# A two-layer hybrid backbone with experts: rooms of 32 rows for the two lightest experts of the second layer

## The chip, the cores and the metric

One core of one Trainium2 chip. The metric is the device time in us of one execution; a lower one is better. The profiled execution is one such execution, seen by the hardware profiler: its span runs from the first to the last of the program's instructions. TensorE is called PE in the rows, its weight loads PEld, VectorE DVE, ScalarE ACT, GpSimd POOL and SyncE SP.

## What is computed

Two layers over 512 latent tokens and, in the first layer, 256 context tokens, 1024 channels each, all in float32. A layer is a mixer (a bidirectional RWKV branch and a Hyena branch) and then a mixture of experts. The change is in the experts of the second layer, on 512 tokens. Cut to that:

```python
scores = softmax(h @ w_router); sel = scores + router_bias
best_group = argmax over 4 groups of (sum of the group's two best sel)
idx = top 2 of sel inside the best group;  wts = scores[idx] / their sum
y[t] = sum over i in 0, 1 of wts[t, i] * ((silu(h[t] @ w_gate[e]) * (h[t] @ w_up[e])) @ w_down[e])   # e = idx[t, i]
x = layer_norm(ALPHA * x + gate * y)
```

There are 16 experts, each with three matrices of 1024 x 1024, 12.6 MB in float32. All of them are read from HBM, 201 MB in the second layer. Which tokens go to which expert is known only at run time. On these inputs the reference's routing of the second layer gives expert 0 62 tokens and the others, from the heaviest, 170, 114, 90, 75, 75, 74, 60, 55, 47, 44, 39, 33, 29, 29 and 28.

## The kernel before

*Ranks and rooms.* Expert 0 is rank 0 and is computed first. The other 15 are sorted at run time by their number of tokens: rank 1 is the heaviest, rank 15 the lightest. CAPS (L25) gives each rank a room, a fixed number of rows; in the second layer 64 for rank 0, 192, 128, five times 96 (ranks 3 to 7) and eight times 64 (ranks 8 to 15). Tokens that find no place in their expert's room go to blocks of 128 rows, each computed by a loop at the end (`overflow`), which runs as often as there are such blocks: here not at all. NOVF (L68) is the most of such blocks that any routing can need.

*Turns.* TURN (L26) says which ranks are computed together. The second layer has seven turns: rank 0 alone (T0), then rank 1 with the pair (15, 14) (T1), 2 with (13, 12) (T2), 3 with (11, 10) (T3), 4 with 5 (T4), 6 with 7 (T5), and the pair (9, 8) (T6). The two experts of a pair share one unit of rows: one gather, one tile of operands, one write of results. A unit has at most 128 rows, so rank 1 with 192 rows is two units. In a turn the experts go forward in six steps: gate, up, gate, up (each for one half of the hidden channels), then two down steps (each for one half of the output channels). Each expert of the turn does one chunk of the step after the other; a chunk reads one block of weights of 1024 x 512.

*Weights.* A chunk's block comes as two halves of 1 MB (`weights`, L2145, tile `raw`), one DMA each from SyncE's queue, into ten buffers in turn (RAW, L23). SyncE's queue is in order: a half is asked for when its buffer is free and when the semaphore that will tell of its landing is free again; every half is read once. So the weights are a stream of 192 halves in the order of the turns.

*Matmuls.* The stationary operand is 128 channels x w rows of tokens, the moving one the weights, in float32. Pieces of 128 rows use the whole array. A piece of 64 rows puts the two halves of the moving columns into two column groups of the array, and one of 32 rows four quarters into four (L1997); in a down chunk the column groups take turns over the contraction instead (L2000). A 96-row expert is a piece of 64 and one of 32. The trace shows two matmul records for each call, as float32 takes. The results of gate and up are multiplied and transposed back (`turned`, L2043). After a down chunk the column groups have to be added up: `total` copies one half of the partitions (ScalarE, L2053) and adds it to the other (VectorE, L2054); for 32 rows it does so a second time (L2058, L2059). Then the rows are scaled (L2119).

*Results.* In all turns but the last the rows are written to a buffer in DRAM by ScalarE's queue (yd<-y, L2126), in rooms of 128 rows a unit. The last turn's are added through a matmul with a selection matrix (L2094, L2095), and while it runs GpSimd gathers each token's rows from the DRAM buffer (`early`, L1821). The rooms' unused rows in that buffer are set to zero at the start (`zero_unused`, L684). Operands of a turn are gathered by GpSimd (xg<-hd,idx, L1921) and transposed by TensorE (L1939) in the turn before.

*What sets the order.* Every engine runs its own list of instructions in order; the list is fixed when the program is built, and the build may move an instruction past others that do not depend on it. The two pieces of a 96-row expert, one after the other in the code, alternate by half chunks in the trace.

Of the kernel before, what the change touches and what calls it, by code (L numbers as in the profile page):

```python
# [8 lines left out]
F32 = mybir.dt.float32  # L9
# [3 lines left out]
ALU = mybir.AluOpType  # L13
# [8 lines left out]
NTOK, NCTX, NLAT = 768, 256, 512  # L22
RAW = 6, 10  # L23
AHEAD = 2, 2
CAPS = ([96] + [256] + [192] + [160] * 3 + [96] * 3 + [64] * 7, [64] + [192] + [128] + [96] * 5 + [64] * 8)  # L25
TURN = ([((0,),), ((1,), (15, 14)), ((2,), (13, 12)), ((3,), (11, 10)), ((4,), (6,)), ((5,), (7,)), ((8,), (9,))],  # L26
        [((0,),), ((1,), (15, 14)), ((2,), (13, 12)), ((3,), (11, 10)), ((4,), (5,)), ((6,), (7,)), ((9, 8),)])
LATE = 1, 1
XLO = (1, 3), ()
EARLY_V = ()  # L30
# [11 lines left out]
def most_overflow(caps, slots, most):  # L42


    seen = {}

    def go(r, n, left):
        if r < 1:
            return 0
        key = (r, n, left)  # L50
        if key not in seen:
            best = 0
            for b in range(0, (most - caps[r] + 127) // 128 + 1):
                m = max(n, caps[r] + 128 * (b - 1) + 1 if b else 0)
                if m > min(most, left):
                    break
                best = max(best, -(-max(0, m - caps[r]) // 128) + go(r - 1, m, left - m))
            seen[key] = best
        return seen[key]

    best = 0
    for b in range((most - caps[0] + 127) // 128 + 1):
        m = caps[0] + 128 * (b - 1) + 1 if b else 0
        best = max(best, b + go(len(caps) - 1, 0, slots - m))
    return best


NOVF = (most_overflow(CAPS[0], 2 * NTOK, NTOK), most_overflow(CAPS[1], 2 * NLAT, NLAT))  # L68


def rows_of(l):


    base, q, first = {}, 0, 0
    cut = max(0, len(TURN[l]) - LATE[l])
    for i, group in enumerate(TURN[l]):
        first = q if i == cut else first
        for ranks in group:
            for j, r in enumerate(ranks):
                base[r] = 128 * q + 64 * j  # L80
            q += -(-CAPS[l][ranks[0]] // 128)
    return [base[r] for r in range(16)], q, first


NSB = tuple(rows_of(l)[1] for l in range(2))
P_BMOD, P_MU, P_W0, P_A0, P_KK, P_KA, P_RK, P_CW, P_CB, P_HB, P_LG, P_LB, P_NG, P_NB = 0, 48, 63, 71, 79, 83, 87, 91, 127, 139, 143, 147, 151, 159
NPAR = 167
# [36 lines left out]
def shape_constants():  # L124
# [47 lines left out]
    for l in range(2):  # L172
        caps[:, l, 0] = CAPS[l]
        caps[:, l, 1] = rows_of(l)[0]
# [404 lines left out]
class Kern:  # L579
# [37 lines left out]
    def setup(self):  # L617
# [40 lines left out]
        self.hd = self.dt_([NTOK, 1024], "hd")  # L658
        self.xd = self.dt_([6, 128, 1024], "xd")
        self.yd = [self.dt_([128 * rows_of(l)[2] + 1, 1024], f"yd{l}") for l in range(2)]  # L660

    def layer(self, l):
# [21 lines left out]
    def zero_unused(self, pool):  # L684
# [4 lines left out]
        for l in range(2):  # L689
            base, nsb, first = rows_of(l)  # L690
            used = {(b + 32 * i) // 32 for b, c in zip(base, CAPS[l]) for i in range(c // 32)}
            for q in range(4 * first):
# [908 lines left out]
    def moe(self, l, st):  # L1601
# [5 lines left out]
        nb = 6 - b0  # L1607
        caps = CAPS[l]
        nblk = [-(-c // 128) for c in caps]
# [344 lines left out]
    def expert(self, l, P, evs, units, xs):  # L1954
# [4 lines left out]
        nc, A = self.nc, self.A  # L1959
        tt, stt = nc.vector.tensor_tensor, nc.vector.scalar_tensor_tensor  # L1960
        n = len(evs)
        pieces = []
        for u, (rows, *_) in enumerate(units):
            split = self.splits(l, rows, n)
            if n == 2:
                pieces += [(u, 64, 64 * j, j, False) for j in range(2)]
            elif rows == 128:
                pieces.append((u, 128, 0, 0, split))
            else:
                pieces += [(u, 64, 0, 0, False)] * (rows >= 64) + [(u, 32, rows // 64 * 64, 0, False)] * (rows % 64 > 0)  # L1970
# [78 lines left out]

        def total(a, w, o):  # L2050

            t = P["a"].tile([128, 512], F32, name="sum", tag="y", bufs=3)[o:o + 64]
            nc.scalar.copy(t, a[64 - o:128 - o])  # L2053
            tt(t, a[o:o + 64], t, ALU.add)  # L2054
            if w == 64:
                return t
            v = P["a"].tile([128, 512], F32, name="sum", tag="y", bufs=3)[o:o + 32]
            nc.scalar.copy(v, t[32:64])  # L2058
            tt(v, t[0:32], v, ALU.add)  # L2059
            return v  # L2060

        def select(u):
# [38 lines left out]
        def down(h, j):  # L2101
            H = slice(512 * h, 512 * h + 512)

            def done(acc):
                for u, (rows, _, own, dst, _) in enumerate(units):
                    if j == 0:
                        out[u] = P["a"].tile([128, 512], F32, name="y", tag="yw", bufs=YW[l])
                        if l == 0:
                            g[u] = P["a"].tile([128, 512], F32, name="g", tag="act", bufs=ACT_BUFS[l])
                            stt(g[u][0:rows], self.grow[1][0:rows, H], own[:, 2:3], self.grow[0][0:rows, H], ALU.mult, ALU.add)  # L2110
                        else:
                            g[u] = self.grow[0][:, H]
                for (u, w, o, *_), a in zip(mine[j], acc):
                    rows, _, own, dst, _ = units[u]
                    R = slice(o, o + w)
                    y, by = out[u][R], own[R, 1:2]
                    if w < 128:
                        a = total(a, w, o)
                    stt(y, a, by, g[u][R], ALU.mult, ALU.mult)  # L2119
                if j < n - 1:  # L2120
                    return
                for u, (rows, _, own, dst, _) in enumerate(units):
                    if dst is None:
                        add(u, h)
                    else:
                        nc.scalar.dma_start(dst[:, H], out[u][0:rows])  # L2126
            return done
# [94 lines left out]
```

## Time and profile before

| | us |
|---|---|
| three runs, median (lowest, highest) | 3251.6 (3239.0, 3257.0) |
| profiled execution | 3243.5 |
| its span | 3241.7 |
| TensorE busy | 2926.6, 90% |
| VectorE, ScalarE, GpSimd busy | 1661.5, 1119.7, 569.0 |
| T1 to T6 and close of the second layer's experts | 538 |

A busy TensorE is not one at its peak: matmuls are pipelined, and the records of the four column groups lie over each other. A group of rows by form gives busy time as the union of its records, so busy time by count is what one record adds. A wait for several semaphores is put down to the one that came last.

### The profile page before, as it was taken

The numbers are of one execution on the slowest core, as the hardware profiler recorded it, in microseconds if no ns is written. First come the engines' busy times: TensorE is split into PE (matmuls) and PEld (weight loads), VectorE is DVE, ScalarE is ACT, GpSimd is POOL, SyncE is SP. The second block draws the span as 40 slices with busy tenths as digits, with TensorE's granted clock in tenths as the row PEclk, the third lists the DMA queues.
The fourth block names the chain that finished last, engine by engine and source line by source line (L and its number), as shares of the span: only waits on it lengthen the run. The fifth ranks groups of instructions, "written<-read, shape, count | busy, mean of one in ns | idle before, by whom it ended". The sixth has DMA issues, their size and how long they took to land. (4 is left out here: it accounts for less than half of the span.)

```text
span 3241.7 us, 60246 instructions
## 1 busy us (share of the span) xinstructions
PE 2926.6 (90%) x24658; PEld 2002.0 (62%) x24658; DVE 1661.5 (51%) x2971; ACT 1119.7 (35%) x2275; POOL 569.0 (18%) x456
## 2 busy tenths in 40 slices
PE   7999999888988799999997999989989879999994
PEld 5877866676777566555652867646666665444551
DVE  4466534887766544435645347446886570111223
ACT  3454225656421133333422444254564221111110
POOL 1001222444004200000022001254440030000002
PEclk8999999899999799999997899987999979999998
DMA  5453274111244689998895464451112549999996
GB/s 223 126 155 103 80 257 143 45 54 49 100 136 169 244 341 367 361 361 320 320 359 213 150 200 120 158 173 57 42 59 75 188 189 377 362 410 421 379 374 248
DMA packets 221345, 689.49 MB, mean 213 GB/s; under 512 B 71877, under 2 KB 99814, under 8 KB 169608
## 3 DMA queue, kind: packets, MB, share of 16 engines
q1 hardware_dynamic: 186280, 587.57, 49.2%
q10 hardware_dynamic: 26960, 71.65, 6.3%
q0 software_dynamic: 7824, 26.36, 2.2%
q8 instruction: 197, 3.23, 0.4%
q14 instruction: 84, 0.69, 0.1%
HBM read 621.20 MB, written 64.30 MB: 211 GB/s over the span
## 5 line engine op out<-in xcount | busy, mean ns | idle before, releaser
L1997 PE MATMUL acc<-raw,x 128*64 128x256 f32 (+2 forms) x6656 | 556.4, 339 | 19.9 <-DMA raw<-in_w_exp 19.6
L1997 PEld LDWEIGHTS acc<-raw,x 128*64 128x64 f32 (+2 forms) x6656 | 344.7, 126 | 219.6 <-issue 89.4
L588 DVE TENSOR_TENSOR lo<-raw,hi 128x1024 fp32r<-128x1024 f32 x190 | 229.8, 1232 | 300.6 <-ACT hi L587 293.3
L2000 PE MATMUL acc<-raw,a 128*64 128x512 f32 (+2 forms) x1312 | 285.9, 605 | 10.4 <-DMA raw<-in_w_exp 7.6
L587 ACT CAST hi<-raw 128x1024 fp32r<-128x1024 f32 x190 | 193.4, 1048 | 289.2 <-PE px L856 157.9
L2028 DVE TENSOR_TENSOR act<-acc,act 128x256 f32<-128x256 f32 (+2 forms) x94 | 40.9, 435 | 432.3 <-PE acc L1997 389.4
L852 PE MATMUL pl<-xh,hi 128*128 128x512 f32 x560 | 227.4, 406 | 0.2
L857 PE MATMUL pl<-xh,lo 128*128 128x512 f32 x560 | 223.4, 399 | 0.3 <-DVE lo L588 0.3
L853 PE MATMUL pl<-xl,hi 128*128 128x512 f32 x560 | 223.6, 399 | 0.0
L2000 PEld LDWEIGHTS acc<-raw,a 128*64 128x64 f32 (+2 forms) x1312 | 77.6, 131 | 178.4 <-issue 155.3
L1132 PE MATMUL gp<-gx,raw 128*128 128x512 f32 (+1 forms) x352 | 175.3, 615 | 0.7 <-ACT gs L1134 0.5
L1921 POOL DMA_INDIRECT xg<-hd,idx x31 | 30.8, 994 | 773.7 <-PE pt L1939 702.1
L852 PEld LDWEIGHTS pl<-xh,hi 128*128 128x128 f32 x560 | 106.0, 189 | 44.9 <-issue 21.1
L2023 ACT ACTIVATE act<-acc 128x256 f32<-128x256 f32 (+2 forms) x94 | 37.0, 393 | 239.3 <-PE acc L1997 204.5
L2048 ACT COPY a<-pt 128x256 f32<-128x256 f32 (+2 forms) x82 | 28.0, 353 | 258.4 <-PE pt L2043 258.4
L857 PEld LDWEIGHTS pl<-xh,lo 128*128 128x128 f32 x560 | 106.6, 190 | 16.9 <-issue 8.7
L2054 DVE TENSOR_TENSOR sum<-acc,sum 64x512 f32<-64x512 f32 x78 | 53.6, 687 | 123.5 <-ACT sum L2053 122.9
L853 PEld LDWEIGHTS pl<-xl,hi 128*128 128x128 f32 x560 | 106.5, 190 | 13.4 <-issue 5.9
L310 PE MATMUL pO<-T,K 128*128 128x192 f32 (+1 forms) x320 | 85.5, 381 | 28.5 <-DVE T L329 26.9
L855 PE MATMUL px<-xh,hi 128*128 128x256 f32 x376 | 109.8, 293 | 0.0
L2053 ACT COPY sum<-acc 64x512 f32<-64x512 f32 x78 | 45.3, 581 | 183.9 <-PE acc L2000 183.8
L856 PE MATMUL px<-xl,hi 128*128 128x256 f32 x376 | 108.3, 289 | 0.1
(605 smaller groups left out, 6176.2 us busy)
## 6 DMA issues: line engine op xcount, KB each, us to landing
raw<-in_w_exp SPq DMA_DIRECT2D x384, 1024.0 KB
mraw<-in_w_mod SPq DMA_DIRECT2D x64, 512.0 KB
raw<-in_w_in SPq DMA_DIRECT2D x36, 512.0 KB
rkk<-rkk SPq DMA_DIRECT2D x24, 768.0 KB
raw<-in_w_in ACTq DMA_DIRECT2D x34, 512.0 KB
mraw<-in_w_mod SPq DMA_DIRECT2D x12, 1024.0 KB
raw<-in_w_in SPq DMA_DIRECT2D x32, 256.0 KB
wb<-in_w_branch SPq DMA_DIRECT2D x32, 256.0 KB
```

Of the source, the lines that this page charges most:

```text
L310: nc.tensor.matmul(pO[:, jj, 0:192], lO, T[c][kO, j, 1, :], start=True, stop=True)
L587: self.nc.scalar.copy(hi, src)
L588: (engine or self.nc.vector).tensor_tensor(lo, src, f32(hi), ALU.subtract)
L852: mm(pl, hi[:, k], xh[:, k, L], start=f, stop=False)
L853: mm(pl, hi[:, k], xl[:, k, L], start=False, stop=False)
L855: mm(px, hi[:, k], xh[:, k, X], start=f, stop=False)
L856: mm(px, hi[:, k], xl[:, k, X], start=False, stop=False)
L857: mm(pl, lo[:, k], xh[:, k, L], start=False, stop=e)
L1132: nc.tensor.matmul(p[:, :n], raw[k // 4][:, k % 4], self.gx[:, k, a - T0:a - T0 + n], start=k == 0, stop=k == 7)
L1997: mm(a[w * g:w * g + w, 0:4 * w], x, raw[:, 4 * w * g:4 * w * g + 4 * w], start=k == 0, stop=k == 7)
L2000: mm(a[w * g:w * g + w], x, raw, start=k < G, stop=k >= 8 - G)
L2054: tt(t, a[o:o + 64], t, ALU.add)
```

## The change

The two lightest ranks, 14 and 15, get rooms of 32 rows, and rank 7 one of 64 instead of 96. The pair (15, 14) thus is one unit of 64 rows whose experts use four column groups each. T4 becomes (4), (7) and T5 (5), (6). Three places that had 64 rows for an expert of a pair written into them now take the room's size: the base of the pair's second expert, its pieces, and `total`, which for 32 rows now works at any offset of 32. NOVF of the second layer becomes 14 instead of 13.

```diff
-CAPS = (..., [64] + [192] + [128] + [96] * 5 + [64] * 8)
+CAPS = (..., [64] + [192] + [128] + [96] * 4 + [64] * 7 + [32] * 2)
 TURN = ([...],
-        [((0,),), ((1,), (15, 14)), ((2,), (13, 12)), ((3,), (11, 10)), ((4,), (5,)), ((6,), (7,)), ((9, 8),)])
+        [((0,),), ((1,), (15, 14)), ((2,), (13, 12)), ((3,), (11, 10)), ((4,), (7,)), ((5,), (6,)), ((9, 8),)])
...
-                base[r] = 128 * q + 64 * j
+                base[r] = 128 * q + CAPS[l][r] * j
...
-                pieces += [(u, 64, 64 * j, j, False) for j in range(2)]
+                pieces += [(u, rows // 2, rows // 2 * j, j, False) for j in range(2)]
...
-            t = P["a"].tile([128, 512], F32, name="sum", tag="y", bufs=3)[o:o + 64]
-            nc.scalar.copy(t, a[64 - o:128 - o])
-            tt(t, a[o:o + 64], t, ALU.add)
+            b = o // 64 * 64
+            t = P["a"].tile([128, 512], F32, name="sum", tag="y", bufs=3)[b:b + 64]
+            nc.scalar.copy(t, a[64 - b:128 - b])
+            tt(t, a[b:b + 64], t, ALU.add)
             if w == 64:
                 return t
             v = P["a"].tile([128, 512], F32, name="sum", tag="y", bufs=3)[o:o + 32]
-            nc.scalar.copy(v, t[32:64])
-            tt(v, t[0:32], v, ALU.add)
+            nc.scalar.copy(v, t[32 - o + b:64 - o + b])
+            tt(v, t[o - b:o - b + 32], v, ALU.add)
             return v
```

## Rows read from the trace of the kernel before

**Rows 1.** The page: granted TensorE clock, in tenths, in 40 slices.

```profile
PEclk8999999899999799999997899987999979999998
```

**Rows 2.** Busy time, clock, DMA share, GB/s of seven stretches: turns T1 to T6, close.

```profile
core 0: us, PE busy (x) PEld busy (x) DVE busy (x) ACT busy (x) POOL busy (x), PEclk, DMA share, GB/s
2703.70:2813.70 110.00, 110.00 (x613) 55.09 (x612) 14.01 (x22) 12.24 (x26) 1.83 (x2) 1.00 0.94 361
2813.70:2906.50 92.80, 90.10 (x452) 42.99 (x452) 10.33 (x16) 9.80 (x20) 1.82 (x2) 1.00 1.01 412
2906.50:2997.20 90.70, 83.47 (x802) 42.50 (x799) 16.58 (x27) 13.95 (x31) 0.94 (x1) 1.00 1.01 421
2997.20:3070.60 73.40, 73.40 (x926) 38.05 (x926) 14.64 (x26) 13.02 (x30) 0.00 (x0) 1.00 0.94 382
3070.60:3143.40 72.80, 72.80 (x922) 37.28 (x918) 17.04 (x29) 13.46 (x30) 0.00 (x0) 1.00 0.91 366
3143.40:3205.50 62.10, 45.62 (x326) 23.28 (x324) 12.57 (x19) 6.58 (x14) 26.13 (x16) 1.00 0.98 401
3205.50:3241.70 36.20, 7.06 (x24) 2.69 (x24) 21.58 (x41) 3.29 (x7) 0.00 (x0) 0.61 0.16 59
```

**Rows 3.** The same view, columns as above, inside T1 (three) and T4 (two).

```profile
2735.00:2765.00 30.00, 30.00 (x178) 16.19 (x176) 0.85 (x2) 3.25 (x8) 0.00 (x0) 1.00 0.96 384
2765.00:2793.00 28.00, 28.00 (x164) 13.39 (x164) 5.30 (x9) 2.77 (x6) 0.00 (x0) 1.00 0.91 344
2793.00:2813.70 20.70, 20.70 (x88) 8.26 (x84) 5.32 (x8) 3.89 (x7) 1.83 (x2) 1.00 0.84 296
2997.20:3053.00 55.80, 55.80 (x825) 33.73 (x827) 4.99 (x12) 7.15 (x20) 0.00 (x0) 1.00 1.01 420
3053.00:3070.60 17.60, 17.60 (x105) 4.33 (x101) 9.66 (x15) 5.86 (x11) 0.00 (x0) 1.00 0.69 262
```

**Rows 4.** Whom SyncE's queue waited for in T3: us in total, times, longest.

```profile
SPq L2145 <- DMA raw<-in_w_exp: 55.2, 25, 6.0
SPq L2145 <- DMA yd<-y: 23.5, 3, 11.0
```

**Rows 5.** The same in T4.

```profile
SPq L2145 <- DMA yd<-y: 28.0, 3, 13.8
```

**Rows 6.** TensorE in order of time, end of T3: start, us, what, idle before.

```profile
2991.55 1.94 PE L2000 MATMUL acc<-raw,a 128*64 128x512 f32 x8 [0.61 <-DMA raw<-in_w_exp]
2997.15 1.70 PE L1997 MATMUL acc<-raw,x 128*64 128x256 f32 x13 [1.28 <-DMA raw<-in_w_exp]
```

**Rows 7.** Matmuls of T1 by form: count, busy us, mean ns, idle before.

```profile
L1997 PE MATMUL acc<-raw,x 128*64 128x256 f32 x384 | 42.8, 381 | 0.0
L2000 PE MATMUL acc<-raw,a 128*64 128x512 f32 x97 | 21.9, 595 | 0.0
L2043 PE MATMUL pt<-con,act 128*128 128x128 f32 x20 | 3.4, 286 | 0.0
```

**Rows 8.** The same in T4, 32-row pieces.

```profile
L1997 PE MATMUL acc<-raw,x 128*32 128x128 f32 x512 | 17.3, 276 | 0.0
L2000 PE MATMUL acc<-raw,a 128*32 128x512 f32 x64 | 8.5, 605 | 0.0
```

**Rows 9.** ScalarE in order of time: the first write of T4's rows.

```profile
3056.04 0.33 ACTq L2126 DMA_DIRECT2D yd<-y  x1
```

**Rows 10.** The second fold of 32-row pieces, whole stage, by form.

```profile
L2059 DVE TENSOR_TENSOR sum<-sum 32x512 f32<-32x512 f32 x10 | 6.8, 683 | 6.8 <-ACT sum L2058 6.8
L2058 ACT COPY sum<-sum 32x512 f32<-32x512 f32 x10 | 6.1, 613 | 9.9 <-DVE sum L2054 9.9
```

**Rows 11.** DMA issues, 2690 to 3200 us: count, KB each, median us to landing.

```profile
raw<-in_w_exp SPq DMA_DIRECT2D x175, 1024.0 KB
xg<-hd,idx POOLq DMA_INDIRECT x8, 10.5
```

**Rows 12.** GpSimd's writes of zeros: duration ns min/median/max, first and last start.

```profile
L696 POOL DMA_DIRECT2D yd<-zero x28: 496/507/742, 417.8 to 444.0; - x28
```

More of the change, by code (lines that the diff above doesn't have):

```diff
@@ L24 @@
 AHEAD = 2, 2
-CAPS = ([96] + [256] + [192] + [160] * 3 + [96] * 3 + [64] * 7, [64] + [192] + [128] + [96] * 5 + [64] * 8)
+CAPS = ([96] + [256] + [192] + [160] * 3 + [96] * 3 + [64] * 7, [64] + [192] + [128] + [96] * 4 + [64] * 7 + [32] * 2)
 TURN = ([((0,),), ((1,), (15, 14)), ((2,), (13, 12)), ((3,), (11, 10)), ((4,), (6,)), ((5,), (7,)), ((8,), (9,))],
-        [((0,),), ((1,), (15, 14)), ((2,), (13, 12)), ((3,), (11, 10)), ((4,), (5,)), ((6,), (7,)), ((9, 8),)])
+        [((0,),), ((1,), (15, 14)), ((2,), (13, 12)), ((3,), (11, 10)), ((4,), (7,)), ((5,), (6,)), ((9, 8),)])
 LATE = 1, 1
```

## Prediction

> **What bounds the kernel now.** I read the page's clock line first (near full speed in the last fifth, where the experts of the second layer are [rows 1]), then one stretch per turn of the second layer's experts [rows 2] (T1 to T6 are its first six rows, and its last row is what follows the last half), since the change touches nothing else that costs time. In [rows 2] the reader should hold two columns together: TensorE is busy over 90% of the time in T1 to T5, and the DMA rate stands between 361 and 421 GB/s. The stage is a race between two conveyors. One is the weight stream: 192 halves of 1024 KB, asked for in order by SyncE's queue [rows 11]; at 421 GB/s, the rate that the third turn holds [rows 2], a half takes 1.049 MB / 421 = 2.49 us. The other is TensorE, which consumes six halves in a step of a turn with a pair (14.94 us of stream) and four in a step of two experts (9.96 us). Ten buffers couple them.
>
> The stream has to carry the same halves whatever TensorE does, so what counts is the time in which it ran under 421: length x (1 - rate/421) from [rows 2]. T1: 110 x 60/421 = 15.7 us. T2: 2.0. T3: 0. T4: 6.8. T5: 9.5. T6: 2.9. In T1 a step takes 110/6 = 18.3 us against 14.94, in T4 73.4/6 = 12.2 against 9.96, in T5 12.1: there TensorE is the slower conveyor, the buffers stay full and the stream stands. In T3 the stream is the slower one: TensorE waits 0.6 to 1.3 us for the last halves [rows 6]. Only the 35 us or so of lost stream can be won; the 36.2 us behind the last half are not touched.
>
> Where in a turn the stream stands matters too. In T4 it holds 420 GB/s through the four gate and up steps and falls to 262 in the two down steps; T1 gives 384, 344 and 296 [rows 3]. In T4 SyncE waited up to 13.8 us at once for writes of finished rows (yd<-y) to land, 28.0 us in all [rows 5]; the first of T4's writes was issued only at 3056.0 [rows 9], 59 us into the turn. So the queue that fetches weights stands behind output writes, and those come late in a turn. T3 has such waits too, 23.5 us with up to 11.0 in one, and loses nothing [rows 4]: the halves asked for before are still on their way when the write lands. The wait costs only where TensorE lags behind the stream.
>
> **The change, part by part.** *The pair's matmuls (T1).* A 64-row chunk is 32 matmul records, in two column groups: 42.8/384 x 32 = 3.57 us for gate and up, 21.9/97 x 16 = 3.61 us for down [rows 7]. A 32-row chunk is 64 records of half the columns, in four groups: the 32-row pieces of T4 give 17.3/512 x 64 = 2.16 us and 8.5/64 x 16 = 2.13 us [rows 8]. Eight gate and up chunks save 8 x 1.41 = 11.3, four down chunks 4 x 1.48 = 5.9, and four transposes fewer at 3.4/20 = 0.17 us [rows 7] 0.7: together 17.9 us. The bounds: 0 if four groups bring nothing in this place, and 22 if a chunk costs half of what it did (in T4 the pieces alternate with 64-row ones, and each change of width is in their price). I take 18, the row of the same shape. T1 becomes 92 us, 15.3 a step against 14.94 of stream.
>
> The Trainium skill speaks against this: "TensorE: Matmul & The Clock Gate", section "Wait — 56ns, not 53.3ns?", gives about 62 ns to issue a matmul where the sequencer decodes in software; 64 records would then take an estimated 4.0 us and the chunk would get dearer than its 3.57. By that T1 would get some 3 us longer, an estimate, and the gain of the whole sum shrink to some 9 us. The trace does not agree: 33.8 ns a record in T4 [rows 8].
>
> *Its sums.* Four groups need a second fold: one more copy of 613 ns and one more add of 683 ns for each of four down chunks [rows 10], 5.2 us on ScalarE and VectorE, which are busy 12.2 and 14.0 us of T1's 110 [rows 2]. Nothing on TensorE waits for them soon; what does is the pair's write and, behind it, SyncE's queue. So each of the pair's two writes comes 1.3 us later behind its chunk, though the chunk itself ends earlier.
>
> *The seventh expert in T4 instead of a 96-row one, (5) and (6) in T5.* The 32-row pieces of one expert go: 4 x 2.16 + 2 x 2.13 = 12.9 us and two transposes, 13.2 in all [rows 7, 8]. T4 becomes 60.2 us, 10.0 a step against 9.96. T5 keeps two 96-row experts, and T6 is as before.
>
> *Bytes.* 64 rows fewer are gathered and written for the pair, 32 for the seventh expert, 4 KB each: 0.79 MB, 1.9 us of stream.
>
> *Small things.* Two more blocks of zeros are written at the start of the kernel, at about 507 ns of GpSimd each [rows 12]; GpSimd is busy 18% there, and without that cover they would cost 1 us. One more possible overflow block lengthens a few small tables by 1 in 25: nothing I can see, at most 0.1 us. The waits on the gather: the pair's is shorter; the median gather lands after 10.5 us [rows 11], and I count no gain.
>
> **The sum.** T1: the gate and up steps nearly fit the stream, so their 2.6 us (30 x 37/421, [rows 3]) come back. The down steps lost 28 x 77/421 + 20.7 x 125/421 = 11.2; there SyncE still stands behind the writes. The bounds are T3, which loses 0 with steps as long as the stream's, and T4, 6.8 with steps 2.2 us too long; T1's new steps are 0.4 too long but it starts with full buffers, which is to say with TensorE lagging. I leave 5 lost, and also the 1.9 of T1's first 31 us. So T1 gives 8.8. T2 starts with less lag: of its 2.0 I take 1. T3 is bound by the stream and passes all this on: its end comes about 10 us earlier. TensorE can follow: T1 to T3 were 293.5 us and need 275.5. T4 then starts without lag, as before, but its steps fit the stream: 6.8 come back. T5 no longer starts with full buffers; it starts as T4 did, with the same two shapes, so it loses what T4 lost: 9.5 - 6.8 = 2.7 come back. T6 waits for the stream, as before. With 1.9 of bytes: 8.8 + 1 + 6.8 + 2.7 + 1.9 = 21.2 us.
>
> The profiled execution took 3243.5 us; the change would make it 3222.3. It lies 8.1 under the median of the three runs, 3251.6 (3239.0 to 3257.0). I set the forecast on the middle of the two, 3247.6: **3226 us**.
>
> **The rivals.** *All of it comes back* (chance 0.13). If SyncE's waits for writes cost nothing once TensorE is quick, T1 gives 13.9, T2 2.0, T4 6.8, T5 9.5, bytes 1.9: 34 us, 3214. For it: T3's waits are free. Against it: T5 has the same two shapes as T4 had.
>
> *T1's part stays lost* (0.20). The fold puts the pair's write 1.3 us later, TensorE begins T1 behind full buffers, and SyncE waits for the write before it asks for T2's halves; then T1 gives nothing and the rest 12.4: 3235. For it: the drop to 296 GB/s is in T1's last step [rows 3]. Against it: TensorE's part of each down step ends 3 us earlier. The skill's page "TensorEngine Tiling (Array Packing)", section "PSUM Bottleneck", has this rule: tiling speeds up the matmuls but not the evacuation of PSUM. No row of before shows a pair that is folded twice.
>
> *Four groups bring nothing, or the stream's loss is not due to TensorE* (0.08). Then only T4's lighter expert or the bytes are left: 2 to 8 us, 3240 to 3246.
>
> *Slower: a room is too small* (0.05). The rooms hold 32, 32 and 64 rows; the reference's routing on these inputs gives 28, 29 and 60 tokens to the two lightest and the seventh, so it should hold, by 3 tokens in one place. From 33 tokens on an expert gets a block after the end: a gather of 10.5 us [rows 11], twelve halves fetched with nothing ahead, 12 x 2.49 = 29.9, and the closing work again, 36.2 [rows 2]: 77 us, net +55, 3303.
>
> **How the numbers follow.** The forecast (gain of 17 to 27 us) has 0.54. The range: from the full gain on the lowest run (3239 - 33) to T1's part lost on the median with some spread: 3206 to 3244; outside lie the slower rival, part of the fourth and the far spread. What a measurement can tell from no change is about 0.5%, 16 us. Faster by more: 0.13 + most of 0.54 = 0.65. Within: T1's part lost, nothing gained and the low edge of the forecast: 0.29. Slower: 0.06.
>
> **What would show it.** Right: T1 about 92 us at over 400 GB/s, with pair records of 128x128 at 34 ns each; T2 and T3 at 415 or more; T4 about 60 us at 415 with TensorE waiting for halves in it; T5 about 73 us with its drop near 262 GB/s in the down steps; T6 some 65 us. Wrong: T1 shorter by 18 but T2 or T3 longer by the same with the rate in T1's down steps still under 350 (T1's part lost); T5 at 421 (all of it back); a clock under 1.00 in T1 to T5, which the turns of before do not show [rows 2], T6's repeated waits included; work behind the closing rows (a room too small).

## The result

| us | kernel before | changed kernel | ratio, 95% interval |
|---|---|---|---|
| first comparison, 3 runs each: median (lowest, highest) | 3251.6 (3239.0, 3257.0) | 3208.8 (3208.0, 3215.4) | 0.9896 (0.9864 to 0.9928) |
| repeated, 25 and 5 runs | 3242.6 (3230.5, 3259.1) | 3221.9 (3218.7, 3243.7) | 0.9930 (0.9906 to 0.9954) |
| profiled execution of the first comparison; its span | 3243.5; 3241.7 | 3208.8; 3207.0 | |
| in it, start of T1 | 2703.7 | 2689.0 | |
| in it, start of T1 to the end | 538.0 | 517.9 | |

The kernel became faster, by some 20 us or 0.6%. The first comparison shows 43 us, and its two profiled executions 34.7. Of these 34.7, 20.1 lie behind the start of T1, where the change is; the other 14.7 lie ahead of it, in work that both kernels share but for two blocks of zeros and a shorter gather. They are scatter: in the later profile of the changed kernel T1 starts at 2722.0, in that of the kernel before at 2715.9, and over the fourteen profiles of this study, in which the work ahead of T1 differs in little (some writes of zeros, the gather of the pair's rows, the queue of T0's writes, in two of them one weight buffer fewer), it starts between 2683.9 and 2722.0. So the distance from the start of T1 to the end is the quantity that I compare from here on, with the ratios of the timed runs beside it.

The changed kernel by turns, in one view: busy time and count of each engine, clock, DMA share and GB/s; the first six rows are T1 to T6, the last is the close, as in [rows 2].

```profile
core 0: us, PE busy (x) PEld busy (x) DVE busy (x) ACT busy (x) POOL busy (x), PEclk, DMA share, GB/s
2689.04:2781.91 92.87, 91.55 (x865) 47.06 (x864) 14.03 (x23) 12.92 (x29) 1.82 (x2) 1.00 1.00 397
2781.91:2877.99 96.08, 90.67 (x452) 42.59 (x449) 12.56 (x20) 11.28 (x23) 1.83 (x2) 1.00 1.02 413
2877.99:2972.43 94.44, 84.40 (x799) 42.67 (x799) 16.28 (x27) 13.04 (x30) 0.94 (x1) 1.00 1.01 421
2972.43:3035.20 62.77, 60.56 (x635) 31.47 (x637) 11.07 (x20) 10.11 (x23) 0.00 (x0) 1.00 1.01 416
3035.20:3107.97 72.77, 72.77 (x919) 37.26 (x915) 15.84 (x27) 12.84 (x29) 0.00 (x0) 1.00 0.94 378
3107.97:3170.80 62.83, 45.71 (x326) 23.44 (x324) 13.27 (x20) 6.57 (x14) 26.58 (x16) 1.00 0.98 406
3170.80:3207.00 36.20, 6.75 (x24) 2.62 (x20) 21.29 (x40) 3.29 (x7) 0.00 (x0) 0.61 0.16 59
```

Read it against [rows 2]. T1 went from 110.0 to 92.9 us and from 361 to 397 GB/s. T2 and T3 became longer, 96.1 and 94.4 after 92.8 and 90.7: TensorE no longer comes into them behind full buffers and now waits for halves. The three together are 283.4 us after 293.5. T4 went from 73.4 to 62.8 at 416 GB/s, and TensorE is idle 2.2 us in it. T5 is as long as before, all of it TensorE. T6 and the close, 99.0 together, were 98.3.

The same columns inside the changed kernel's turns: T1's two down steps, then T5's gate and up steps and its down steps.

```profile
2750.40:2766.70 16.30, 16.13 (x74) 6.00 (x73) 2.86 (x4) 3.42 (x7) 0.92 (x1) 1.00 1.01 390
2766.70:2781.90 15.20, 15.20 (x73) 5.11 (x72) 6.35 (x9) 3.33 (x7) 0.91 (x1) 1.00 0.92 346
3035.20:3087.00 51.80, 51.80 (x801) 32.19 (x797) 4.92 (x11) 5.66 (x17) 0.00 (x0) 1.00 1.01 416
3087.00:3108.00 21.00, 21.00 (x121) 5.09 (x119) 10.95 (x16) 7.18 (x13) 0.00 (x0) 1.00 0.77 286
```

T1's down steps now hold 390 and 346 GB/s where [rows 3] had 344 and 296. T5 has taken the shape that T4 had: 416, then 286 [rows 3].

Matmuls of T1 by form in the changed kernel (count, busy us, mean ns, idle before).

```profile
L1997 PE MATMUL acc<-raw,x 128*32 128x128 f32 x512 | 15.6, 274 | 0.0
L1997 PE MATMUL acc<-raw,x 128*64 128x256 f32 x128 | 14.7, 382 | 0.0
L2000 PE MATMUL acc<-raw,a 128*64 128x512 f32 x33 | 8.1, 601 | 0.0
L2000 PE MATMUL acc<-raw,a 128*32 128x512 f32 x64 | 7.7, 598 | 0.0
```

A gate and up chunk of the pair is 15.6/512 x 64 = 1.95 us, a down chunk 7.7/64 x 16 = 1.93; they were 3.57 and 3.61 [rows 7].

Whom SyncE's queue waited for in the changed kernel (us in total, times, longest): first in T1, then in T4.

```profile
SPq L2146 <- DMA yd<-y: 38.4, 6, 14.6
SPq L2146 <- PE acc L1997: 38.2, 21, 9.0
```

```profile
SPq L2146 <- DMA raw<-in_w_exp: 33.2, 15, 4.4
SPq L2146 <- DMA yd<-y: 15.6, 2, 8.9
```

In T4 the queue now waits mostly for its own halves, which is what a stream at its rate looks like, and 15.6 us for writes where [rows 5] had 28.0. In T1 the writes still hold it up, once for 14.6 us, from 2754.2 to 2768.9, behind T1's first write, which ScalarE issued only at 2762.0. Over most of that time the halves asked for before are still on their way (DMA share 1.02 up to the write's issue, 0.79 from 2765.0 on). A later wait, of 5.0 us, stands in the chain of waits of the changed kernel, at the end of T1 (start, us, what):

```profile
2766.77 11.67 PE acc L2000 x40
2778.46 0.59 ACT sum L2054
2779.07 0.69 DVE sum L2055
2779.79 0.76 DVE y L2120
2780.57 6.40 DMA yd<-y
2787.07 10.06 DMA raw<-in_w_exp
2797.26 8.98 PE acc L1997 x32
```

At this place the kernel before has a chain of TensorE alone. Now it runs through T1's last write but one: fold, scaling and write, 8.6 us, stand ahead of a half that T2 needs and for which TensorE waits 0.6 us.

### The profile page after: what moved, and what is told of

Same layout as the page of the kernel before. It is cut to its first block, busy times and chain, and to the rows that moved or that the text cites. A ratio compares the mean times of both kernels' runs of the same rounds, so it can differ in the third digit from the quotient of the medians.

```text
span 3207.0 us, 60151 instructions
## 1 busy us (share of the span) xinstructions
PE 2890.7 (90%) x24620; PEld 1982.6 (62%) x24620; DVE 1654.3 (52%) x2967; ACT 1115.8 (35%) x2271; POOL 570.6 (18%) x458
## 3 DMA queue, kind: packets, MB, share of 16 engines
q1 hardware_dynamic: 186280, 587.57, 49.8%
## 5 line engine op out<-in xcount | busy, mean ns | idle before, releaser
L1997 PE MATMUL acc<-raw,x 128*64 128x256 f32 (+2 forms) x6656 | 541.6, 336 | 23.0 <-DMA raw<-in_w_exp 16.8
L1997 PEld LDWEIGHTS acc<-raw,x 128*64 128x64 f32 (+2 forms) x6656 | 337.6, 125 | 216.2 <-issue 101.1
L2000 PE MATMUL acc<-raw,a 128*64 128x512 f32 (+2 forms) x1280 | 275.4, 605 | 8.2 <-DMA raw<-in_w_exp 7.8
L857 PEld LDWEIGHTS pl<-xh,lo 128*128 128x128 f32 x560 | 106.9, 191 | 18.4 <-issue 10.1
L853 PEld LDWEIGHTS pl<-xl,hi 128*128 128x128 f32 x560 | 106.7, 191 | 13.8 <-issue 6.2
L859 PE MATMUL px<-xh,lo 128*128 128x256 f32 x376 | 107.8, 288 | 0.0
```

The source lines that it names most:

```text
L853: mm(pl, hi[:, k], xl[:, k, L], start=False, stop=False)
L857: mm(pl, lo[:, k], xh[:, k, L], start=False, stop=e)
L859: mm(px, lo[:, k], xh[:, k, X], start=False, stop=e)
L1997: mm(a[w * g:w * g + w, 0:4 * w], x, raw[:, 4 * w * g:4 * w * g + 4 * w], start=k == 0, stop=k == 7)
L2000: mm(a[w * g:w * g + w], x, raw, start=k < G, stop=k >= 8 - G)
```

## The experiments

One table first, since all are read alike. "Lost" is the measure of my prediction, length x (1 - rate/421), for each turn of each kernel's profile (by unrounded rates, so that a few figures of before differ by 0.1 from the prediction's); "T1 to end" is from T1's first matmul to the end of the span; "close" is what follows the last half of weights. Each ratio is against 19 to 25 runs of the kernel before, that of `changed` against 3.

The measure counts every stretch under 421, and not all of it is a stream that stands. In T1's last down step of the changed kernel the DMA share is 0.92: there it stands. In T2 it does not. Its first 79 us in the changed kernel and its last 17, then its last 15.5 before the change and its last 17 in `write_gpsimd_after`, a run in which SyncE waits for no write (below):

```profile
2781.91:2861.00 79.09, 75.45 (x402) 37.53 (x400) 8.70 (x14) 9.54 (x20) 1.83 (x2) 1.00 1.02 421
2861.00:2877.99 16.99, 15.22 (x54) 5.06 (x51) 3.86 (x6) 1.74 (x3) 0.00 (x0) 1.00 1.02 376
```

```profile
2891.00:2906.50 15.50, 15.50 (x58) 5.64 (x56) 3.62 (x5) 1.16 (x2) 0.00 (x0) 1.00 1.02 364
```

```profile
2882.00:2899.20 17.20, 15.76 (x58) 5.40 (x55) 4.06 (x6) 1.74 (x3) 1.16 (x2) 1.00 1.02 368
```

All of T2's loss lies in its last step, and the DMA engines are busy through it: they move fewer bytes in the same time. The gather of T3's operands and two writes are in flight there; which of them makes the transfers slower is not shown, and T3, with a gather of its own, runs at 421. T1 has such a part too: 1.3 us in its first 31 us (404 GB/s at a share of 1.02) and 1.2 in its first down step (390 at 1.01), so of its 5.3 us 2.7 are a stream that stands.

| kernel | lost in T1, T2, T4, T5, T6 | T4, T5 long | close | T1 to end | ratio, 95% |
|---|---|---|---|---|---|
| before | 15.7, 2.0, 6.9, 9.6, 3.0 | 73.4, 72.8 | 36.2 | 538.0 | |
| again_before | 16.5, 2.1, 6.7, 9.5, 2.6 | 73.4, 72.8 | 36.3 | 537.7 | 0.9996 (0.9982 to 1.0011) |
| changed | 5.3, 1.8, 0.7, 7.4, 2.1 | 62.8, 72.8 | 36.4 | 517.9 | 0.9896 (0.9864 to 0.9928) |
| again_after | 6.1, 2.2, 0.8, 7.7, 2.1 | 63.8, 72.8 | 36.6 | 519.9 | 0.9930 (0.9906 to 0.9954) |
| pair_only | 5.6, 1.8, 7.5, 9.6, 2.8 | 73.4, 72.8 | 36.8 | 529.1 | 0.9952 (0.9933 to 0.9970) |
| seventh_only | 15.6, 2.0, 0.4, 6.8, 2.5 | 62.7, 72.8 | 36.6 | 527.8 | 0.9978 (0.9958 to 0.9998) |
| old_turns | 5.4, 2.0, 6.8, 2.0, 3.3 | 73.2, 60.6 | 36.6 | 520.6 | 0.9936 (0.9918 to 0.9954) |
| write_gpsimd_before | 11.9, 2.5, 0.2, 7.1, 4.9 | 74.3, 72.8 | 38.9 | 529.8 | 0.9951 (0.9931 to 0.9970) |
| write_gpsimd_after | 3.6, 2.2, 0.1, 1.3, 4.7 | 63.0, 72.8 | 42.8 | 519.1 | 0.9920 (0.9893 to 0.9948) |
| three_turn | 6.2, 1.8, 1.2, 5.4, 0.1 | 64.4, 96.2 | 49.8 | 528.2 | 0.9946 (0.9922 to 0.9971) |
| write_gpsimd_v45 | 3.4, 2.1, 0.1, 0.6, 12.3 | 63.2, 72.8 | 48.2 | 531.0 | 0.9958 (0.9937 to 0.9979) |
| write_gpsimd_v5 | 3.4, 2.2, 0.1, 1.3, 16.0 | 63.0, 72.8 | 49.0 | 536.2 | 0.9984 (0.9963 to 1.0005) |
| balanced_nine | 4.2, 1.7, 0.4, 0.7, 3.2 | 63.2, 61.8 | 46.6 | 524.8 | 0.9965 (0.9944 to 0.9985) |
| balanced_nine_write | 2.8, 2.0, 0.1, 0.1, 4.3 | 63.1, 62.2 | 51.9 | 529.0 | 0.9971 (0.9943 to 0.9999) |

### Both kernels again

No edit. The question was whether the first comparison's 43 us, twice the forecast gain, are the change's.

> The kernel before, unchanged, for the scatter of what lies ahead of T1. In the two profiles T1 begins at 2703.7 us (before) and 2689.0 (after), and from there to the end it is 538.0 and 518.0. Theory (the 14.7 us ahead of T1 are scatter between executions): T1 begins anywhere from about 2685 to 2715, ratio 1.000 with an interval of some 0.3%, and T1 to the end is 538 within 1 us. Rival (the change itself shortens what is ahead): T1 begins at 2704 within 4 us.

> The changed kernel, unchanged. Theory of scatter: T1 to the end is 518 within 1 us, T1 begins anywhere from 2685 to 2715, and the ratio lies at (3247.6 - 20)/3247.6 = 0.994 within 0.003. Rival (ahead of T1 is shortened by the change): T1 begins at 2689 within 4 us and the ratio is 0.989 again.

Behind the start of T1 the pair of profiles repeats to 2 us: 537.7 and 519.9, a gain of 17.8 after 20.1; 519.9 lies just outside the 518 within 1 us that I had expected. Ahead of it nothing repeats: T1 starts at 2715.9 and 2722.0, somewhat above the expected 2685 to 2715, and this time the changed kernel's T1 starts 6.1 us later than that of the kernel before. With 25 and 5 runs the ratio is 0.9930, which is 22.7 us, between 15 and 30. So the change is worth about 19 us, and the rest of the first comparison was scatter.

### Each part alone

`pair_only` takes the rooms of 32 rows and leaves T4 to T6; `seventh_only` takes the seventh rank's room and the new T4 and T5. Both have the changed kernel's forms of the base, the pieces and `total`.

```diff
# pair_only, against the kernel before
-[64] + [192] + [128] + [96] * 5 + [64] * 8
+[64] + [192] + [128] + [96] * 5 + [64] * 6 + [32] * 2
# seventh_only, against the kernel before
-[64] + [192] + [128] + [96] * 5 + [64] * 8
+[64] + [192] + [128] + [96] * 4 + [64] * 9
-((4,), (5,)), ((6,), (7,)), ((9, 8),)
+((4,), (7,)), ((5,), (6,)), ((9, 8),)
```

> The two lightest in rooms of 32, the seventh expert and the turns as before. By the forecast's sum T1 falls from 110.0 to 92 us with some 5 us of its stream lost, T2 and T3 are bound by the stream; T4 keeps two 96-row experts (73.4 us) and loses about 6.8 of stream, T5 loses 9.5 as before: T1 to the end about 538 - 8.8 - 1 - 1.2 (bytes) = 527. Rival (all of T1's loss comes back): 522. Rival (T1's part stays lost): 537.

> The pair keeps rooms of 64; the seventh expert has 64 and computes with the fourth, the fifth with the sixth. By the forecast's sum T1 to T3 stay as before (293.5 us), T4 falls from 73.4 to 61 us and loses no stream, T5 takes T4's place and loses 7 instead of 9.5: T1 to the end about 538 - 6.8 - 2.5 - 0.6 (bytes) = 528. Rival (T5 gives it back: its buffers fill, and it loses what T4 and T5 lost together): 537.

T1 and T4 of `pair_only`, then T1, T4 and T5 of `seventh_only`, columns as above:

```profile
2701.70:2794.62 92.92, 91.55 (x865) 47.08 (x864) 14.03 (x23) 12.90 (x29) 1.82 (x2) 1.00 1.00 396
2986.10:3059.52 73.42, 73.42 (x925) 38.09 (x925) 14.70 (x26) 13.00 (x30) 0.00 (x0) 1.00 0.93 378
```

```profile
2704.18:2814.21 110.03, 110.03 (x613) 55.09 (x612) 14.01 (x22) 12.24 (x26) 1.82 (x2) 1.00 0.94 362
2997.24:3059.97 62.73, 60.55 (x634) 31.48 (x636) 11.03 (x20) 10.12 (x23) 0.00 (x0) 1.00 1.01 419
3059.97:3132.75 72.78, 72.78 (x919) 37.26 (x915) 15.85 (x27) 12.86 (x29) 0.00 (x0) 1.00 0.95 382
```

Each part changes its own turn and leaves the other's as it was. Against the mean of the two profiles of before, 537.9, the pair gives 8.8 us and the seventh rank 10.1; together 18.9, and the changed kernel gives 20.0 and 18.0. The parts add up, as the ledger of lost stream says they should. That they add up also speaks against the rival by which T1's part stays lost: alone it brings 8.8.

### The new rooms with the old turns

```diff
-((4,), (7,)), ((5,), (6,)), ((9, 8),)
+((4,), (5,)), ((6,), (7,)), ((9, 8),)
```

> All three rooms as in the changed kernel, but the fourth expert computes with the fifth and the sixth with the seventh, as before. Theory (a turn with steps longer than the stream's costs only what the ten buffers can't hold, wherever it stands): T4 has two 96-row experts and starts without lag, 73.4 us, losing about 7 of stream; T5 starts with full buffers but needs only 10.0 us a step, so it loses 1 to 4 in its start instead of 9.5; T1 to the end 516 to 521, as with the new turns (518 and 520). Rival (pairing the seventh with the fourth is what saves T4's loss, and with the old turns T4 and T5 keep the 16 they lost): 527 to 530.

T1 to end is 520.6, that is 2.7 and 0.7 more than in the two profiles of the changed kernel, and the ratios' intervals lie over each other. The loss simply moves: T4 keeps its 6.8, T5 has 2.0 instead of 7.4. So the gain of the second part comes from the seventh rank's lighter room; in which of the two turns it sits is not seen to matter. "Turns paired anew" is worth nothing that these runs can tell.

### The writes from another queue

If SyncE stands because of writes of finished rows, the loss in a turn whose TensorE lags should go when the writes no longer come from ScalarE's queue.

```diff
-nc.scalar.dma_start(dst[:, H], out[u][0:rows])
+(nc.gpsimd if l else nc.scalar).dma_start(dst[:, H], out[u][0:rows])
```

> The kernel before, but the second layer's finished rows are written from GpSimd's queue instead of ScalarE's. Theory (in the down steps SyncE's queue stands behind those writes, as both take turns on the same landing semaphores): no wait of SyncE on yd is left, T4, whose lag is under the buffers' 25 us, loses 0 to 2 of stream instead of 6.8, T1 and T5, which start with full buffers, keep most of theirs; T1 to the end 526 to 533. Rival (the buffers alone make the loss): 537 to 538. Rival (GpSimd's queue, where gathers stand before the writes, delays the writes): longer than 538.

> The changed kernel with the second layer's finished rows written from GpSimd's queue. Theory: the drop in T1's down steps (390 and 346 GB/s) was SyncE's wait for writes, 14.6 us in one; it goes, T1 loses 0 to 2 instead of 5.3, T5 loses 3 to 7 instead of 7.4; T1 to the end 509 to 515. Rival (the buffers alone): 518 to 520. Rival (GpSimd's gathers delay the writes): longer.

SyncE's waits of `write_gpsimd_before` in T4 (us in total, times, longest), the two largest, and that kernel's T4:

```profile
SPq L2145 <- DMA raw<-in_w_exp: 21.7, 12, 3.7
SPq L2145 <- PE acc L1997: 11.9, 6, 2.3
```

```profile
2985.64:3059.98 74.34, 73.49 (x925) 38.07 (x925) 15.22 (x26) 13.00 (x30) 2.10 (x4) 1.00 1.01 420
```

In the kernel before, the wait of 13.8 us [rows 5] runs from 3047.7 to 3061.5, and the write that ended it was issued at 3056.0 [rows 9]: for 8.3 us SyncE waits for a transfer that has not begun. In the traces ScalarE's writes signal their landing on the same eight semaphores as the halves of weights, and GpSimd's on eight others. With the writes moved no wait for a write is left, in T4 or in any other turn, and T4 loses 0.2 us instead of 6.9 with the same matmuls as before (420 GB/s over a turn whose down steps had 262 [rows 3]). That is the cause that I read from [rows 5], shown: not TensorE's lag by itself, but the writes for which the queue waits, late in the turn. Its other half is shown by T1, which with the writes moved still loses 11.9 us: there TensorE is 3.4 us a step slower than the stream, and the buffers are full (376 and 341 GB/s in the middle steps, at DMA shares of 0.94 and 0.90).

In the changed kernel the same edit does what it should to the stream, and the end does not come sooner. T1 to T5 lose 7.3 us instead of 15.4, the last half lands 476.2 us after T1's start instead of 481.5, and T1 to end is 519.1 after 517.9 and 519.9. I had expected 509 to 515, and that was wrong. So was the reading that both of T1's down steps had dropped because of the writes: they go from 390 and 346 GB/s to 390 and 395, and T1 still loses 3.6 us, at DMA shares of 1.01 to 1.02. Of the 8.1 us won up to T5's end, T6 gives back 2.6. Where the rest went is seen at the end. VectorE's additions of finished rows in `write_gpsimd_after`, in order of time (start, us, what, idle before), then GpSimd's last addition of gathered rows there, then T6 and the close:

```profile
3179.99 2.59 DVE L2120 SCALAR_TENSOR_TENSOR y<-sum,own,g 64x512 f32<-64x512 f32 x1
3183.26 2.09 DVE L588 TENSOR_TENSOR yl<-y,yh 128x512 fp32r<-128x512 f32 x1 [0.68 <-ACT yh L587]
```

```profile
3181.98 2.82 POOL L1831 TENSOR_TENSOR xs<-a,xs 128x1024 f32<-128x1024 f32 x1
```

```profile
3129.20:3186.47 57.27, 44.38 (x312) 23.89 (x308) 12.74 (x15) 6.00 (x13) 27.20 (x17) 0.94 0.94 387
3186.47:3229.31 42.84, 11.59 (x37) 3.90 (x36) 24.33 (x45) 3.87 (x8) 0.00 (x0) 0.62 0.13 50
```

And the same two of VectorE, and GpSimd's last, in the changed kernel:

```profile
3164.54 0.75 DVE L2120 SCALAR_TENSOR_TENSOR y<-sum,own,g 64x512 f32<-64x512 f32 x1
3165.97 0.69 DVE L588 TENSOR_TENSOR yl<-y,yh 128x512 fp32r<-128x512 f32 x1 [0.68 <-ACT yh L587]
```

```profile
3161.13 2.79 POOL L1831 TENSOR_TENSOR xs<-a,xs 128x1024 f32<-128x1024 f32 x1
```

T5 is all TensorE and ends 418.9 and 419.0 us after T1's start. GpSimd gathers each token's rows when T5's rows are written, and its additions end 55.9 us after T5's end in the one and 55.6 in the other. With the better stream the last expert's rows meet these additions instead of following them: VectorE's two steps take 2.59 and 2.09 us instead of 0.75 and 0.69. (In the changed kernel the rows of the expert before meet them, 2.27 us at 3159.4, while TensorE waits for halves anyway.) The Trainium skill has a rule for that on its page "SBUF — State Buffer", section "SBUF: two separate sides": VectorE, when it reads two operands from SBUF, and GpSimd exclude each other from a common pair of ports for the length of an instruction; the two rows agree with it: the second ends 0.55 us after GpSimd's last addition. TensorE waits 2.4 us for the cast of the first of these results. The granted clock is at the lower of its two levels, 1.2 GHz, from 3176.1 to 3179.5, after TensorE had waited 1.8 to 2.0 us for each of three halves, and from 3182.9 to 3189.8, after the wait for the cast; there eight matmuls take 3.51 us instead of 1.94. Over T6 that is 0.94, where the changed kernel keeps 1.00. So TensorE's last down matmul ends 8.3 us behind the last half instead of 3.5. How much of these 4.8 us is VectorE's longer steps and how much the clock, no run here separates.

The close takes 42.8 us instead of 36.4, and some 2.0 of that has nothing to do with the additions. GpSimd's last long instruction, a drain behind the closing rows, takes 8.97 us instead of 7.01 (times, then shortest, median and longest in ns; first `write_gpsimd_after`, then the changed kernel):

```profile
L2219 POOLq DRAIN  x3: 46/103/8971, 3219.5 to 3229.0; - x3
```

```profile
L2219 POOLq DRAIN  x3: 46/103/7011, 3199.1 to 3206.7; - x3
```

All five kernels that write from GpSimd's queue have this: 8.8 to 9.1 us, after 6.9 to 7.3 in the nine others. So the gain of the stream is given back in T6 and the close, in part to a cost of the move itself.

### T5 longer, T6 shorter

If GpSimd's work behind T5 takes part in setting the end, T5's end should come earlier relative to the stream, or its cost be spread. The first try put one expert of the last pair into T5.

```diff
-((5,), (6,)), ((9, 8),)
+((5,), (6,), (8,)), ((9,),)
```

> The changed kernel with T5 of three experts, (5), (6) and (8), and (9) alone in the last turn. TensorE's step in T5 is then about 16 us against 14.94 of stream instead of 12.1 against 9.96, so the buffers hold the lag and T5 loses 0 to 3 of stream instead of 7.4; the last turn has 12 halves instead of 24 and the token gathers of GpSimd, 26 us of its work, have to fit beside 30 us of stream. Theory: T1 to the end 511 to 518. Rival (GpSimd's gathers and adds end last and set the end): 520 to 530.

T1 to end is 528.2, as the rival had it. T6 is short, 32.3 us, and the last half lands 478.4 us after T1's start; but GpSimd starts its gathers only when T5 is done, and now that is 32.3 us before the last half instead of 62.6. Its last addition:

```profile
3191.34 2.33 POOL L1831 TENSOR_TENSOR xs<-a,xs 128x1024 f32<-128x1024 f32 x1
```

It ends at 3193.7, 15.2 us behind the last half (3178.5), and the close is 49.8 us. In this kernel the chain of waits runs from T5's last write through the gathers and GpSimd's additions to the close: with T5 so long, the end hangs on T5's end plus GpSimd's work.

### VectorE for some of GpSimd's additions

With the writes on GpSimd's queue, the additions of the last two blocks (`write_gpsimd_v45`), or of the last (`write_gpsimd_v5`), go to VectorE.

```diff
-EARLY_V = ()
+EARLY_V = (4, 5)
...
-op = nc.vector.tensor_tensor if tb in EARLY_V else nc.gpsimd.tensor_tensor
+op = nc.vector.tensor_tensor if l and tb in EARLY_V else nc.gpsimd.tensor_tensor
```

> The changed kernel with writes from GpSimd's queue, and the last turn's additions of gathered rows for two of four token blocks on VectorE instead of GpSimd. With the writes moved alone, the last half landed 476.2 us after T1's start instead of 481.5 and 483.3, but the close behind it took 42.8 instead of 36.4 and 36.6: GpSimd's additions ran until 3184.8, into the last chunks, VectorE's records beside them took 2.6 and 2.1 us instead of 0.8 and 0.7, and TensorE fell to the lower clock before its last chunk. Theory (the close got longer because GpSimd's additions end too late): they end some 9 us earlier, the last half at 476, the close 36 to 38, T1 to the end 512 to 514. Rival (the additions on VectorE stand in the way of the last turn's chunks): T1 to the end 518 or more.

> As the other, with one block of four on VectorE. Theory: GpSimd's additions end some 5 us earlier, the close 36 to 39, T1 to the end 512 to 516. Rival: 518 or more.

VectorE and TensorE in T6 of `write_gpsimd_v45`, in order of time:

```profile
3158.39 3.31 DVE L1830 TENSOR_TENSOR x<-x 128x1024 f32<-128x1024 f32 x1 [29.80 <-DMA x<-yd,slot]
3161.74 0.42 DVE L2028 TENSOR_TENSOR act<-acc,act 128x256 f32<-128x256 f32 x1
```

```profile
3162.22 0.69 PE L2043 MATMUL pt<-con,act 128*128 128x128 f32 x2 [27.11 <-DVE act L2028]
```

VectorE's list is in order, and the addition stands ahead of the product that T6's matmuls need; it waits 29.8 us for gathered rows, TensorE 27.1 us behind it, and the stream loses 12.3 us. T1 to end is 531.0 and, with the last block alone, 536.2. The rival was right twice.

### One of the last pair into T5, one into T6

T4 to T6 then have two experts each. A second selection matrix is needed, and one of the ten weight buffers makes room for it.

```diff
-RAW = 6, 10
+RAW = 6, 9
-((4,), (7,)), ((5,), (6,)), ((9, 8),)
+((4,), (7,)), ((5,), (8,)), ((6,), (9,))
-SOME, YB, YW = 4, 1, (3, 3)
+SOME, YB, YW = 4, 2, (3, 3)
-name="sel", tag="sel", bufs=1
+name="sel", tag="sel", bufs=2
```

`balanced_nine_write` has the writes on GpSimd's queue besides.

> The changed kernel with every late turn of one 96-row and one 64-row expert: (4) with (7), (5) with (8), (6) with (9), so that no step after T3 is longer than the stream's; room for the second unit of the last turn is taken from the weights' buffers, nine instead of ten. In all runs so far T5 with two 96-row experts took 72.8 us of TensorE and ended 418.9 us after T1's start, with the stream 5 to 7 us better or not. Theory: T5 falls to 61 to 63 us and ends at 407 to 411, T6 with two units is bound by the stream and the token gathers, 66 to 72 us, the close 36 to 39: T1 to the end 511 to 518. Rival (nine buffers lose in T1 and T2 what T5 wins): T1 loses 8 or more of stream instead of 5.3 to 6.1, and T1 to the end is 518 to 523.

> The same with the second layer's rows written from GpSimd's queue. Theory: SyncE no longer stands behind writes, T1 loses 2 to 5 of stream and T5 under 1; T1 to the end 508 to 515. Rival (GpSimd's additions set the end of the last turn, as with the writes moved alone): the close is 40 us or more and T1 to the end no shorter than in the other.

T5, T6 and the close of `balanced_nine`:

```profile
3046.38:3108.22 61.84, 59.95 (x637) 31.33 (x634) 12.23 (x21) 10.39 (x24) 0.00 (x0) 1.00 1.01 416
3108.22:3176.33 68.11, 58.26 (x592) 30.31 (x588) 11.62 (x18) 7.97 (x19) 26.67 (x16) 0.95 0.98 402
3176.33:3222.95 46.62, 19.50 (x64) 6.99 (x60) 27.67 (x49) 5.57 (x11) 0.00 (x0) 0.67 0.12 46
```

T5 did fall to 61.8 us and ends 410.1 us after T1's start instead of 418.9, and no turn from T2 on loses more than 3.2 us of stream; the last half lands at 478.2 instead of 481.5. But the last turn is now two units of rows, and behind the last half 64 matmuls instead of 24 are left, 19.5 us of TensorE instead of 6.8. The close takes 46.6 us, and T1 to end is 524.8 instead of the expected 511 to 518. The rival's reason, nine buffers, is not it: T1 loses 4.2. With the writes moved it is 529.0 with a close of 51.9 us, as that run's rival had it. Turns, selection and buffers changed together here, so their parts are not told apart. No kernel here is clearly ahead of the changed one.

## Why the prediction was right, and where its steps were off

The forecast was 3226 us from a gain of 21.2; the changed kernel took 3208.8 in the first comparison and 3221.9 in the repeated one, both inside the range, and the gain behind T1's start is 20.1 and 17.8. The time of the first comparison lies 17 us under the forecast mainly for a reason that is not in the sum: the scatter ahead of T1. That it is still inside, 2.8 us above the lower edge, owes something to luck; the gain behind T1's start is the test of the sum.

*T1's matmuls.* Forecast 92 us, found 92.9. A chunk of 32 rows costs 1.95 and 1.93 us, less than the 2.16 and 2.13 that I took from T4, perhaps because here the pieces of 32 and of 64 rows do not alternate, which no run tests by itself; but rank 1's 64-row pieces have become dearer, 8.1/33 = 0.245 us a record after 21.9/97 = 0.226 [rows 7]. TensorE's busy time fell by 18.5 (forecast 17.9), and it now waits 1.3 us. A record takes 15.6/512 = 30.5 ns. The time for a matmul decoded in software on the Trainium skill's page "TensorE: Matmul & The Clock Gate", section "Wait — 56ns, not 53.3ns?", by which 64 records would take 4.0 us, is therefore not what binds here; in which way they are decoded no run tells. My estimate from it, T1 some 3 us longer, took the gate and up chunks alone: the down chunks, 16 records each, would by that time still have become shorter.

*What of it comes back.* I left 6.9 us lost in T1; 5.3 and 6.1 are. They are where the forecast put them, in the down steps: 16.3 x 31/421 + 15.2 x 75/421 = 3.9 of the 5.3, against the 5 that I had left there; 1.3 are in the first 31 us, against 1.9. Only the last step's 2.7, at a DMA share of 0.92, are a stream that stands. So the gain in T1 was 10.4, not 8.8.

*T2.* I let 1 of its 2.0 come back: 0.2 did, and -0.1 the second time. This step failed, by its reason too: I had taken the 2.0 us for time in which the stream stood, because the rate was under 421. The lines on T2 above show that it did not stand: the loss is all in T2's last step, at a DMA share of 1.02, before the change as after it, so less lag at T2's start had nothing to give back. With no wait for a write left, T2 loses 2.2. Nor is it the rival "T1's part stays lost": T1's late write, in the chain above, made TensorE wait 0.6 us and left the rate of T2's first 79 us at 421. That chain has the fold of the 64-row piece, a scaling and the write, and not the second fold, which I had named for this rival. The rule of the Trainium skill's page "TensorEngine Tiling (Array Packing)", section "PSUM Bottleneck", that I had weighed with it, shows there only: of the 8.6 us 1.3 are evacuation.

*T4 and T5.* 6.8 and 2.7 were to come back; 6.2 and 2.2 did (5.9 and 1.8 the second time). T4 takes 62.8 us, not 60.2: TensorE fits the stream so well that it is TensorE that waits. Three rows of the changed kernel around T4's start (start, us, what, idle before):

```profile
2969.23 1.94 PE L2000 MATMUL acc<-raw,a 128*64 128x512 f32 x8 [0.45 <-DMA raw<-in_w_exp]
2972.43 9.81 PE L1997 MATMUL acc<-raw,x 128*64 128x256 f32 x128 [1.26 <-DMA raw<-in_w_exp]
2982.80 5.85 PE L1997 MATMUL acc<-raw,x 128*64 128x256 f32 x96 [0.57 <-DMA raw<-in_w_exp]
```

T5 loses 7.4, about as much as T4 did, for T4's reason: it starts without lag, and its down steps meet the writes.

*Bytes.* This term was mis-sized: I took 1.9 us, and it is 0.4 and -0.1. Counted over all transfers of the trace from T1's start to the landing of the last half, the changed kernel moves 195.49 MB after 195.67, 0.18 less, and 195.56 after 195.50 the second time. Of the 0.79 MB the pair's gather, 0.26, lies in T0, ahead of T1; and the changed kernels begin T1 with 0.2 and 0.5 of a half more still to come.

With the terms as found, 10.4 + 0.2 + 6.2 + 2.2 + 0.9 (T6) - 0.1 (T3) + 0.4 = 20.2, and the last half lands 20.3 us earlier behind T1's start (481.5 instead of 501.8); the second time 10.4 - 0.1 + 5.9 + 1.8 + 0.5 - 0.1 - 0.1 = 18.3, and it is 18.1 (483.3 and 501.4). That these terms close is no proof by itself, since loss and bytes make up the length by definition. The forecast's sum held because T1 gave more and T2 and the bytes less.

*The rivals.* All of it coming back, 34 us, did not happen: T1 and T5 keep 5.3 and 7.4. `write_gpsimd_after` shows more than that: where most of this comes back too (T1 to T5 lose 7.3), the end does not move: T5's end stays (418.9 and 419.0), GpSimd's additions follow it by some 56 us, and the move costs 2.0 us at the program's end. My remark that T6 and the close are not touched was true of this change, and hid this. Four groups that bring nothing, and a room too small, are out: T1 fell by 17 us, and nothing follows the closing rows.

What stays open: the ratios of most variants lie somewhat under what T1 to end gives them, by 4 us in the mean of eleven. T1 starts at 2703.7 and 2715.9 in the two profiles of before and at 2683.9 to 2722.0 in the twelve others, so a small difference ahead of T1 can be neither shown nor excluded with one profile of each.

## What to carry to other kernels

Where a stream of weights and a compute engine run against each other, count the time that the stream stands, turn by turn; an engine saving is worth only what of that it gives back, here 19 us for some 30 us of TensorE time, and parts in different turns add up. A rate under the best one is not yet a stream that stands: look at the share of the DMA engines beside it, which told T2's loss from T4's. Before going on with the same lever, look for the next bound: here one more improvement of the stream by 5 us was worth nothing, since work hung on the end of the turn before the last and the move had a price of its own. And when a change shows twice its forecast, compare the distance behind the first instruction that it touches before looking for a mechanism.

## What the runs showed of the hardware

- An in-order queue that fetches weights can stand for 13.8 and 14.6 us because of a write that another engine's queue issues 8.3 and 7.8 us after the wait began, when both kinds of transfer signal on the same semaphores. The same writes from GpSimd's queue, on other semaphores, took all such waits away (104.8 us in 17 waits over T1 to T5 of the changed kernel) and, in the kernel before, T4's lost stream from 6.9 to 0.2 us. GpSimd paid about 0.5 us a write and some 2.0 us more for its last drain.
- The DMA engines can be busy throughout (share 1.02) and move 364 to 376 GB/s instead of 421, as in T2's last step.
- Four column groups with float32 gave 3.57/1.95 = 1.8 times the speed of two for the same chunk, at 30.5 ns a record.
- VectorE's 64x512 operation took 2.59 us beside GpSimd's additions and 0.75 without them.
- The first 2700 us, nearly the same instructions in all fourteen profiles, differed by up to 38 us (2683.9 to 2722.0), in two profiles of the changed kernel by 33 (2689.0 and 2722.0); the last 500 of one and the same kernel differed by 0.3 us (538.0, 537.7) and 2.0 us (517.9, 519.9).
